# A two-layer macaron decoder on one core: closing additions and squares ahead of turned tiles' second parts, copies and later splits; the sixth attention unit split ahead of the seventh

## The chip, the cores and the metric

The kernel runs on one core of a Trainium2 chip. The metric is the device time of one execution in microseconds (us). Engines are named as in the profile: PE (TensorE; PEld its weight loads), DVE (VectorE), ACT (ScalarE), POOL (GpSimd) and SP (SyncE, which issues most transfers).

## What is computed

Two layers over 512 tokens of width 1024, all in float32, and a final RMSNorm:

```python
for l in range(DEPTH):                                   # 2
    x = x + 0.5 * swiglu(rms_norm(x, ffn1_norm[l]), ffn1_wg[l], ffn1_wu[l], ffn1_wd[l])   # 1024 -> 2816 -> 1024
    h = rms_norm(x, mix_norm[l])
    z = h @ w_in[l]                                      # q (8 heads), k, v (2 heads), three conv parts
    attn_out = sliding_window_attention(q, k, v, attn_sink[l])   # window 128, blocks of 128
    conv_out = short_conv(b, c, h_conv, conv_w[l])       # depthwise, 3 taps
    x = x + concatenate([attn_out, conv_out]) @ w_out[l]
    x = x + 0.5 * swiglu(rms_norm(x, ffn2_norm[l]), ffn2_wg[l], ffn2_wu[l], ffn2_wd[l])
return rms_norm(x, final_norm)
```

## The kernel before

**Exact products from split operands.** Every operand of a product is split in two: `hi` is the operand cast to the matmul's type (a cast on ACT, L214), `lo` the rest (a subtraction on DVE, L215). Three matmuls, hi*hi, lo*hi and hi*lo, stand for one. `need_split(g)` makes the splits of weight tiles up to number g into `wh` and `wl` (four buffers each), `take_split()` takes the next one and asks for those three ahead. The raw tiles (512 KB, eight buffers) are loaded four units ahead, mostly from SP's queue (L198, L193), some with an accumulating transfer from POOL (L209).

**Seven products for eight.** The larger products go block by block in seven products over sums of blocks (`seven`, `Seven`, `share`, `winograd`, `winograd2`; `stream` issues the matmuls, L901). `share` runs through a list of seven steps. After a step its accumulators are added to the residual stream `x` in the additions of L951.

**Closing groups.** Where a normalisation follows directly, `share` gets it as `after` and uses the order `CHAINS_EARLY`. Such closings stand at the end of the first feed-forward part of layer 0 and at the end of the mixed part in each layer. There the first two token tiles (half 0) are complete early: each addition that completes a part of `x` is followed by the square of it with a running sum (`Norm.__call__`, L607, ACT). When four have been squared, `Norm.stage` computes the factor: `v` (L631, DVE), a first guess `r` (L632, ACT), three small DVE steps (L514 to L516), and then four scaled tiles `xn` (L641, DVE). `Norm.pull` and `Norm.turn` transpose an `xn` on PE (L665), cast it on ACT (`hh` or `fb`, L674), subtract on DVE (`hl` or `fb`, L675) and, before a feed-forward part, keep a whole copy (`hf`, L677, ACT). In a closing, half 0 is turned between the matmuls of the last step (`z`); the additions of that step complete half 1.

The next part begins on half 0 while half 1 is still normalised: `halves` (after the first closing; PE L333, three weight tiles held) or `plain_halves` (after the mixed parts; PE L1060, four tiles held). Both take their weight tiles first, and `pull` half 1 at fixed places between their matmuls, so PE's order is written out by hand there. The order of DVE and ACT is set by a scheduler from the order in the program; `tc.issue_after(i)` places what is in it behind instruction `i` in that order, without a wait at run time.

**The first feed-forward part of layer 0** has one pair of column blocks done in `winograd`, after a `winograd2`. At the end of `winograd2`, `apart` copies the 16-bit halves of four result tiles into planes on ACT (L1158), `send` has SP transpose them (L1164) and `join` copies them back (L1218) some steps later. At the start of `winograd`, ACT copies the first product `p` out of its accumulator (L1095), and the third step accumulates into the same bank (L1111).

**Attention.** There are eight units, (query block, key head), and each has steps in a table: scores, then either `turn` (transposes on PE, cast L1578, subtraction L1579) or `send` and `join` (planes on ACT L1540, transposed by SP L1547, copied back on ACT L1560, cast `ph` L1564, subtraction `pl` L1566), then `values` (PE, L1590 and L1591). `go_on` does the values, turns, sends and scores of a step, then the next weight split, then the joins:

```python
TURN_AT = (6, None, 8, None, 11, None, 14, 15)
SEND_AT = (None, 7, None, 9, None, 11, None, None)
JOIN_AT = (None, 10, None, 12, None, 14, None, None)
VALUES_AT = (7, 11, 9, 13, 12, 15, 15, 16)
```

The sixth unit is joined in step 14, where the seventh is turned, and both have their values in step 15.

## Time and profile before

| | |
|---|---|
| time, median of 3 runs | 1648.42 us (1647.46 to 1648.55) |
| profiled execution | 1652.75 us, its span 1651.0 us |
| PE busy | 1634.2 us, 99% of the span |
| DVE, ACT busy | 1299.8 us (79%), 1126.2 us (68%) |
| granted PE clock over the span | 0.997 |
| transfers | 308.64 MB, mean 187 GB/s |

The profile is of one execution. Rows of a timeline give start and duration in us, engine, line of the kernel, operation, what is written and read, the count of merged instructions, and in brackets the idle time of the engine before it with what ended that. The durations of PE's matmuls are modelled and overlap; how fast PE runs is read from the distance of their starts. Instructions of DVE and ACT overlap by about 0.1 us as well.

### The profile page before, as it was taken

The page shows a single profiled execution, that of the slowest core. Times are in us where ns is not written, and L with a number is a line of the kernel's source. Part 1 is how long each engine was busy: PE and PEld are TensorE (multiplying, and loading weights), DVE is VectorE, ACT ScalarE, POOL GpSimd, SP SyncE. Part 2 cuts the span into 40 slices and gives each one's busy share as a digit, 9 for nine tenths or more (in the row PEclk, how much of TensorE's full clock was granted, in tenths as well). Part 3 has the DMA queues.
Part 4 walks back from the last instruction along what each step waited for, and adds up shares of the span by engine and source line. Part 5 has one row for each costly group of instructions (what it writes and reads, how often), then busy time and mean ns, then how long its engine had stood idle before and what let it go on. Part 6 is the DMA issues. An engine that isn't in the chain of part 4 may idle for free.

```text
span 1651.0 us, 21081 instructions
## 1 busy us (share of the span) xinstructions
PE 1634.2 (99%) x7576; PEld 1358.5 (82%) x7576; DVE 1299.8 (79%) x1718; ACT 1126.2 (68%) x1581; POOL 193.1 (12%) x172
## 2 busy tenths in 40 slices
PE   9999999999999999999999999999999999999998
PEld 7888888888887888888888888878988878888886
DVE  7987779877798877798788676987577987777885
ACT  7457777557866667786576777865587766777864
POOL 0011111100111111111001111110002101111111
PEclk9999999999999999999999999999999999999999
DMA  9379999932685779999837898997137847999992
GB/s 255 91 190 221 227 210 258 219 91 52 172 198 128 204 193 215 217 228 243 230 83 198 217 217 204 234 242 200 52 90 175 207 114 183 221 219 222 221 259 79
DMA packets 286844, 308.64 MB, mean 187 GB/s; under 512 B 108532, under 2 KB 171028, under 8 KB 286740
## 3 DMA queue, kind: packets, MB, share of 16 engines
q1 hardware_dynamic: 244212, 227.99, 47.4%
q0 software_dynamic: 41824, 78.65, 28.1%
q8 instruction: 59, 0.97, 0.2%
q10 hardware_dynamic: 704, 0.66, 0.1%
q14 instruction: 45, 0.37, 0.1%
HBM read 263.74 MB, written 2.10 MB: 161 GB/s over the span
## 4 chain that ended last, share of the span: by engine, by line
PE 85%; DVE 6%; ACT 4%; DMA 3%; issue 1%; SPq 1%; DVEq 0%; ACTq 0%; POOLq 0%
PE x L901 23%; PE y L901 12%; PE x_s L901 8%; PE w L901 6%; PE y_s L901 4%; PE up L1060 3%; PE down L356 3%; PE acc L306 3%; PE acc L307 3%; PE acc L309 3%; DVE wl L215 2%; PE w_s L901 2%; PE acc L333 2%; DMA raw<-in_ffn_wu_dram 2%; PE x_m L901 1%
## 5 line engine op out<-in xcount | busy, mean ns | idle before, releaser
L215 DVE TENSOR_TENSOR wl<-raw,wh 128x1024 fp32r<-128x1024 f32 (+1 forms) x493 | 595.5, 1214 | 219.2 <-ACT wh L214 216.0
L214 ACT CAST wh<-raw 128x1024 fp32r<-128x1024 f32 (+1 forms) x493 | 511.7, 1044 | 312.9 <-PE y L901 41.3
L901 PE MATMUL x<-wh,ft 128*128 128x512 f32 x608 | 187.1, 389 | 0.0
L901 PE MATMUL y<-wh,ft 128*128 128x512 f32 x608 | 187.1, 389 | 0.0
L901 PE MATMUL x<-wh,fb 128*128 128x512 f32 x608 | 187.1, 389 | 0.0
L901 PEld LDWEIGHTS y<-wh,ft 128*128 128x128 f32 x608 | 114.1, 188 | 23.6
L901 PEld LDWEIGHTS x<-wh,fb 128*128 128x128 f32 x608 | 114.1, 188 | 23.6
L901 PEld LDWEIGHTS x<-wh,ft 128*128 128x128 f32 x608 | 114.1, 188 | 23.6
L901 PE MATMUL x<-wl,fb 128*128 128x512 f32 x304 | 118.3, 389 | 0.0
L901 PE MATMUL x<-wl,ft 128*128 128x512 f32 x304 | 118.3, 389 | 0.0
L901 PE MATMUL y<-wl,ft 128*128 128x512 f32 x304 | 118.3, 389 | 0.0
L1218 ACT COPY raw_a<-pt 128x1024 uint16<-128x1024 uint16 x76 | 103.3, 1359 | 17.1 <-DMA pt<-pl 17.1
L209 POOL DMA_DIRECT2D raw<-in_ffn_wu_dram x39 | 47.3, 1221 | 553.6 <-DMA raw<-in_ffn_wu_dram 373.5
L306 PE MATMUL acc<-hh,wh 128*128 128x512 f32 x240 | 94.6, 394 | 0.0
L307 PE MATMUL acc<-hl,wh 128*128 128x512 f32 x240 | 93.8, 391 | 0.0
L309 PE MATMUL acc<-hh,wl 128*128 128x512 f32 x240 | 93.7, 390 | 0.0
L901 PE MATMUL w<-wh,fb 128*128 128x512 f32 x304 | 93.6, 389 | 0.0
L901 PE MATMUL x_s<-wh,ft_s 128*128 128x512 f32 x256 | 79.0, 390 | 1.0 <-DVE x L951 0.9
L901 PE MATMUL y_s<-wh,ft_s 128*128 128x512 f32 x256 | 78.8, 389 | 0.0
L242 DVE TENSOR_TENSOR raw<-raw,raw 128x1024 f32<-128x1024 f32 x58 | 70.5, 1220 | 9.1 <-DMA raw<-in_ffn_wd_dram 4.9
L209 POOL DMA_DIRECT2D raw<-in_ffn_wg_dram x39 | 47.2, 1217 | 232.3 <-DMA raw<-in_ffn_wu_dram 95.1
L901 PE MATMUL x_s<-wh,fb_s 128*128 128x512 f32 x240 | 73.9, 389 | 0.0
(364 smaller groups left out, 3422.2 us busy)
## 6 DMA issues: line engine op xcount, KB each, us to landing
raw<-in_ffn_wu_dram SPq DMA_DIRECT2D x120, 512.0 KB, 5.2
raw<-in_ffn_wd_dram SPq DMA_DIRECT2D x104, 512.0 KB, 7.0
raw<-in_ffn_wg_dram SPq DMA_DIRECT2D x80, 512.0 KB, 5.1
raw<-in_ffn_wu_dram POOLq DMA_DIRECT2D x39, 512.0 KB, 8.8
raw<-in_ffn_wg_dram POOLq DMA_DIRECT2D x39, 512.0 KB, 6.4
raw<-in_w_in_dram SPq DMA_DIRECT2D x36, 512.0 KB, 4.7
raw<-in_ffn_wd_dram POOLq DMA_DIRECT2D x32, 512.0 KB, 8.5
raw<-raw POOLq DMA_DIRECT2D x20, 512.0 KB, 8.7
```

The source lines that it names most:

```text
L209: nc.gpsimd.dma_start(out=r, in_=rows_of(*more), accum_op=ALU.add)
L214: cast = nc.scalar.copy(hi, raw)
L215: state["sub"] = eng.tensor_sub(lo, raw, f32(hi))
L242: nc.vector.tensor_add(a11, a11, s1)
L306: nc.tensor.matmul(acc, hi[:, k, :], rhs[k][0], start=k == first, stop=False)
L307: nc.tensor.matmul(acc, hi[:, k, :], rhs[k][1], start=False, stop=False)
L309: nc.tensor.matmul(acc, lo[:, k, :], rhs[k][0], start=False, stop=k == last)
L333: nc.tensor.matmul(accs[j][:, t * H : (t + 1) * H], w[:, k, :], x_, start=t + k + i == 0, stop=k == KC - 1 and i == 2, skip_group_check=True,)
L356: nc.tensor.matmul(acc, a[:, k, tok], w[:, k, :], start=i + k + n == 0 and fresh[t], stop=i == last and k == 1 and n == 2, skip_group_chec ...
L901: nc.tensor.matmul(accs[u], x_[:, 2 * h + k, tok], w[:, k, :], start=start and h + k + i == 0, stop=h + k == 2 and i == 2, skip_group_chec ...
L1060: nc.tensor.matmul(accs[t], x_[:, tok], w[:, k, :], start=j + k + i == 0, stop=j == 3 and k == 1 and i == 2,)
L1218: nc.scalar.copy(room.rearrange("p c (n z) -> p c z n", z=2)[:, :, z, :], turned[0][:, NT * z + 2 * c : NT * z + 2 * c + 2, :],)
```

## The change

It makes four moves; the instructions stay the same, and so does PE's order.

- In a closing, the second part of a turned tile is put off. For the first pair of tiles (o = 0) the subtraction stays and the `hf` copy waits; for the second pair (o = 1) both wait. They are kept in `after.later` and issued by `go_on`: subtractions behind the closing additions, `hf` copies behind the squares.
- The weight splits that follow are put later. From step 4 of a closing, `share` asks for one split less ahead; the one of step (6, 1) goes behind the turned subtractions. A new `hold` in `halves` and `plain_halves` places the third held tile's split behind the last closing addition and the fourth's behind the first pair of `xn`.
- `winograd2` ahead of `winograd` (block "u") keeps back the plane copies of its last two tiles until the first product of `winograd` has been copied out.
- `JOIN_AT` keeps the sixth unit alone and is done after the values and before the turns of its step; the second and fourth unit, in `LATE_JOIN_AT`, stay behind the split.

In the order that results, DVE has, before a feed-forward part: two `fb` subtractions, the second held split, the two closing additions, two `fb` subtractions, `v`, the third held split, the rest of the factor, four `xn`, the fourth held split. Before, it had: two held splits, four `fb` subtractions, a held split, the additions, the last held split, `v` and the rest. On ACT the two squares come ahead of the four `hf` copies, two of which stand before the guess `r`. In attention the two join copies of the sixth unit (L1560) move on ACT from behind a later weight cast (`wh`) to between two `ph` casts of the fourth unit, and its `ph` and `pl` ahead of the seventh unit's. On SP one raw load moves ahead of the last two plane transposes of the first feed-forward part; POOL's order stays.

```diff
-JOIN_AT = (None, 10, None, 12, None, 14, None, None)
+JOIN_AT = (None, None, None, None, None, 14, None, None)
+LATE_JOIN_AT = (None, 10, None, 12, None, None, None, None)
...
+    def hold(norm, n):
+
+        first = state["group"]
+        if norm.added:
+            for ahead, one in ((2, norm.added), (3, norm.first)):
+                with behind(one):
+                    need_split(first + ahead)
+        return [take_split(SPLIT_AHEAD - j)[1:] for j in range(n)]
+
     def halves(norm, n, done):
 
         first = state["group"]
-        held = [take_split(SPLIT_AHEAD - j)[1:] for j in range(n)]
+        held = hold(norm, n)
...
             newton(y, r, v)
+            self.first = None
             for o in range(2):
                 xns = []
+                self.first = self.first or (self.scaled if o else None)
...
             nc.scalar.copy(hi, tp)
-            nc.vector.tensor_sub(lo, tp, f32(hi))
-            if not self.mixing:
-                nc.scalar.copy(self.full[o][:, :, tok], tp)
+
+            def rest():
+                self.turned = nc.vector.tensor_sub(lo, tp, f32(hi))
+
+            def keep():
+                if not self.mixing:
+                    nc.scalar.copy(self.full[o][:, :, tok], tp)
+
+            if self.later is None:
+                rest()
+                keep()
+            elif o:
+                self.later.extend(((rest, "added"), (keep, "squared")))
+            else:
+                rest()
+                self.later.append((keep, "squared"))
+
+        def go_on(self):
+
+            for do, behind_ in self.later:
+                with behind(getattr(self, behind_)):
+                    do()
+            self.later = None
...
-                held_back = after and (step, h) == (5, 1)
-                with behind(after.guess, after.scaled) if held_back else nullcontext():
-                    _, wh, wl = take_split(
-                        SPLIT_AHEAD - 1 if after and step in (4, 5) else SPLIT_AHEAD
-                    )
+                held_back = {(5, 1): ("guess", "scaled"), (6, 1): ("turned",)} if after else {}
+                with behind(*(getattr(after, n) for n in held_back.get((step, h), ()))):
+                    _, wh, wl = take_split(SPLIT_AHEAD - 1 if after and step >= 4 else SPLIT_AHEAD)
+                if after and (step, h) == (6, 0):
+                    after.later = []
...
-                            nc.vector.scalar_tensor_tensor(
+                            added = nc.vector.scalar_tensor_tensor(
                                 part, accs[acc][m], by * sign, part, op0=ALU.mult, op1=ALU.add
                             )
                         if after and (step, (o, t)) in ENDS_EARLY:
                             after(2 * t + m, o)
+                        if after and step == 6 and m:
+                            after.added = added
+                            after.go_on()
...
-            held = [take_split(SPLIT_AHEAD - j)[1:] for j in range(4)]
+            held = hold(norm, 4)
...
                     if step == 0:
-                        keep("p1", m, out)
+                        kept_last = keep("p1", m, out)
+                        for lay in pending.pop("u", ()) if m else ():
+                            with behind(kept_last):
+                                lay()
...
             def apart(t):
 
+                if then == "u" and t > 1:
+                    pending.setdefault("u", []).append(lambda: lay(t))
+                else:
+                    lay(t)
+
+            def lay(t):
+
                 planes.append(g2(f"pl_{name}_{t}", U16, (P, 2, S)))
...
-                self.far = JOIN_AT[NT * g + n]
+                self.far = SEND_AT[NT * g + n]
...
-        def attend(step, what=(VALUES_AT, TURN_AT, SEND_AT, SCORES_AT)):
+        def attend(step, what=(VALUES_AT, JOIN_AT, TURN_AT, SEND_AT, SCORES_AT)):
...
-            attend(step - 1, (JOIN_AT,))
+            attend(step - 1, (LATE_JOIN_AT,))
```

More of the change, by code (lines that the diff above doesn't have):

```diff
@@ L116, in g8, with behind @@
         return work.tile(list(shape), dt, tag="g8", bufs=4, name=name)
+    def behind(*those):
+        stack = ExitStack()
+        for one in those:
+            if one is not None:
+                stack.enter_context(tc.issue_after(one.ins))
+        return stack
     def parts_of(name):
@@ L571, in __init__ @@
             self.seen = [0, 0]
+            self.later = self.added = None
             if mixing:
@@ L605, in __call__ @@
         def __call__(self, t, o):
-            nc.scalar.activation(
+            self.squared = nc.scalar.activation(
                 junk(f"sq_{self.i}_{t}_{o}"),
@@ L910, in stream @@
                 norm.pull()
-    def behind(*those):
-        stack = ExitStack()
-        for one in those:
-            stack.enter_context(tc.issue_after(one.ins))
-        return stack
     def share(
@@ L1094, in keep @@
                     kept[what] = g2(f"{what}_{name}", F32, (P, 2, H))
-                nc.scalar.copy(kept[what][:, m, :], src)
+                return nc.scalar.copy(kept[what][:, m, :], src)
             for step, (acc, operand, start) in enumerate(CHAINS):
@@ L1150, in winograd2 @@
             turned = {}
+            then = stages[at + 1][0]
             def apart(t):
+                if then == "u" and t > 1:
[3 more added lines that the diff above has]
+            def lay(t):
                 planes.append(g2(f"pl_{name}_{t}", U16, (P, 2, S)))
@@ L1226, in part @@
                     split(*acts[b + c], raws[b][:, 2 * c : 2 * c + 2, :])
-            gap = 1 if stages[at + 1][0] in "dw" else 2
+            gap = 1 if then in "dw" else 2
             plan = [(1 + n, send, n) for n in range(NT)]
```

## The prediction

> **What bounds the kernel now.** I read the page first, then TensorE's waits, then the timeline of each engine around each wait.

> ```profile
> span 1651.0 us, 21081 instructions
> PE 1634.2 (99%) x7576; PEld 1358.5 (82%) x7576; DVE 1299.8 (79%) x1718; ACT 1126.2 (68%) x1581; POOL 193.1 (12%) x172
> PE 85%; DVE 6%; ACT 4%; DMA 3%; issue 1%; SPq 1%; DVEq 0%; ACTq 0%; POOLq 0%
> ```

> TensorE is busy for 1634.2 of 1651.0 us, and the chain that ended last is 85% its own. The order of its instructions does not move in this change, so all there is to win or lose is its stalls. The view of TensorE's waits (engine, line, releaser; us, times, longest) names them:

> ```profile
> PE xt L665 <- DVE xn L641: 3.8, 3, 1.7
> PE o L1591 <- DVE pl L1566: 1.4, 2, 0.7
> ```

> There are five places: the closing of the mixed part of layer 0 (506 us), of layer 1 (1322 us) and of the first feed-forward part (345 us), where transposes L665 wait for the normalised tiles `xn`; the seventh product step of attention in each layer (445 and 1262 us); and one place in the first feed-forward part (235 us, below). The windows view tells what such a stall costs beside its own length. Its columns are us, then busy time of PE, PEld, DVE, ACT and POOL, then granted clock, DMA share, GB/s:

> ```profile
> 506.90:509.90 3.00, 1.28 (x11) 0.85 (x9) 2.53 (x8) 0.70 (x2) 0.00 (x0) 1.00 1.00 299
> 509.90:514.20 4.30, 4.30 (x15) 3.39 (x13) 1.97 (x4) 1.94 (x4) 2.41 (x2) 0.60 0.59 125
> 1325.90:1330.00 4.10, 4.10 (x13) 3.20 (x12) 1.77 (x3) 1.76 (x3) 2.41 (x2) 0.58 0.47 102
> 235.00:237.00 2.00, 1.01 (x9) 0.80 (x8) 1.76 (x3) 2.00 (x6) 0.00 (x0) 1.00 0.93 253
> ```

> After the two long stalls the granted clock is 0.60 over 4.30 us and 0.58 over 4.10 us: 0.40 x 4.30 = 0.42 x 4.10 = 1.7 us lost each time behind the stall. After the stall of 235 us, which leaves 1.0 us of 2.0 idle, the clock stays at 1.00.

> **The closings of the mixed part.** TensorE in layer 0 (start, us; the x24 and x8 rows are from the chain that ended last and give the undisturbed pace):

> ```profile
> 501.22 0.91 PE L1060 MATMUL up<-wh,fb 128*128 128x512 f32 x2
> 506.76 0.39 PE L1060 MATMUL up<-wl,fb 128*128 128x512 f32 x1
> 508.83 1.29 PE L665 MATMUL xt<-ident,xn 128*128 128x128 f32 x8 [1.68 <-DVE xn L641]
> 515.09 0.71 PE L1060 MATMUL up<-wh,fb 128*128 128x512 f32 x2
> ...
> 514.46 0.87 PE xt L665 x8
> 528.95 5.44 PE x L901 x24
> ```

> A matmul takes 5.44 / 24 = 0.227 us. Between 501.22 and 515.09 lie 36 of them (8.16) and two sets of transposes (1.74), 9.90 us of work in 13.87 us: 3.97 us are lost. In them are 1.84 (508.83 less 506.76 + 0.23), 1.7 for the clock, 0.3 at the start, where the `fb` split is late, and 0.2 where the second `xn` is late. VectorE sets all of this:

> ```profile
> 498.63 2.35 DVE L215 TENSOR_TENSOR wl<-raw,wh 128x1024 fp32r<-128x1024 f32 x2
> 500.89 2.48 DVE L675 TENSOR_TENSOR fb<-xt,fb 128x512 fp32r<-128x512 f32 x4
> 503.29 1.22 DVE L215 TENSOR_TENSOR wl<-raw,wh 128x1024 fp32r<-128x1024 f32 x1
> 504.42 1.28 DVE L951 SCALAR_TENSOR_TENSOR x<-z_m,x 128x512 f32<-128x512 f32 x2
> 505.62 1.22 DVE L215 TENSOR_TENSOR wl<-raw,wh 128x1024 fp32r<-128x1024 f32 x1
> 506.75 0.16 DVE L631 TENSOR_TENSOR v<-ss 128x2 f32<-128x2 f32 x1
> 507.27 0.17 DVE L635 TENSOR_SCALAR v<-v 128x2 f32<-128x2 f32 x1 [0.36 <-ACT r L632]
> 507.93 2.74 DVE L641 SCALAR_TENSOR_TENSOR xn<-x,y,gain 128x512 f32<-128x512 f32 x4
> ...
> 502.15 2.04 ACT L677 COPY hf<-xt 128x512 f32<-128x512 f32 x4
> 506.50 0.19 ACT L607 ACTIVATION_READ_ACCUMULATOR sq<-x 128x1 f32 x1
> ```

> VectorE runs without a gap but the 0.36 us that it waits for ScalarE's `r`. A weight split takes 1.13 from start to start, an `fb` split or an addition 0.60. The changed order after the first split of 498.63 is: two `fb`, the second split, both additions, the other two `fb`, `v`, the third split, then `v`, `y`, `xn`, and only then the fourth split. I lay it out with these durations. The `fb` splits start at 499.76, so the first is done at 500.45, before TensorE asks (501.22): the 0.3 us go. The split follows at 500.96, the additions at 502.09 instead of 504.42, which is 2.33 earlier, the two `fb` at 503.29. The squares end at 506.68 - 2.33 = 504.35. `v` comes at 504.49 and the third split at 504.57, done at 505.79. On ScalarE two `hf` copies (0.5 each) now stand between the squares and `r`: `r` starts at 505.35 and is done by 505.65, still inside the third split, so they cost nothing; that cover is only some 0.1 us, and beyond it each us of ScalarE would be a us of `xn`. The second `v` starts at 505.70 and `xn` 0.66 later, at 506.36 instead of 507.93. Checked in another way: 507.93 less the fourth split (1.13) less the filled wait (0.36) is 506.44.

> What is late next: TensorE, without its 0.3, asks for `xn` at 506.69 and can start 0.15 after the first `xn` ends (507.11), at 507.26. So 0.57 us of the stall stay, and 0.2 us for the second `xn`, which comes 0.67 after the first when four transposes take 0.44. No clock drop is to be expected from 0.8 us, since 1.15 us at 235 us brought none. The third split (505.79) is needed behind the transposes, about 508.6; the fourth, now at 509.05 to 510.27, one tile of 12 matmuls and a set of transposes later, about 512. The buffers these splits free let two loads start later by 1.3 and 3.4 us; the queue behind them next has the transposes of 531 us, so this is nothing. Gain in layer 0: 3.97 - 0.8 = 3.2.

> ```profile
> 1316.77 0.39 PE L1060 MATMUL up<-wh,fb 128*128 128x512 f32 x1
> 1330.88 0.71 PE L1060 MATMUL up<-wh,fb 128*128 128x512 f32 x2
> ```

> Layer 1 loses 14.11 - 9.90 = 4.21. Its `xn` waits are the same to 0.1; I leave it 1.0 and take a gain of 3.2. Both: 6.4 (6.2 to 8.2, the latter if no stall stays).

> **The closing of the first feed-forward part.** Here the second stage works in 256-column matmuls, and the held tiles are wanted sooner:

> ```profile
> 336.26 2.36 DVE L215 TENSOR_TENSOR wl<-raw,wh 128x1024 fp32r<-128x1024 f32 x2
> 343.21 0.28 PE L333 MATMUL acc<-hh,wl 128*128 128x256 f32 x1
> 346.47 1.29 PE L665 MATMUL xt<-ident,xn 128*128 128x128 f32 x8 [0.46 <-DVE xn L641]
> ```

> The loss is 0.46, plus 0.16 because a matmul's modelled end (0.39) overhangs its pace (0.23), plus 0.2 for the second `xn`: 0.8. In the new order: `hl` splits from 337.39, the second split 338.60, additions 339.73, `hl` 340.93, squares done 2.26 after the additions began (506.68 - 504.42), 341.99, but at the latest by 342.3, since ScalarE has a weight cast before them; `v` 342.3, the third split 342.4 to 343.62. TensorE wants that third split at 343.21 and gets it at 343.77: a new stall of 0.56, with `v` and its wait for the squares ahead of it in VectorE's queue. It pushes the transposes back by as much, and `xn` (from 344.2) is then in time. Gain 0.8 - 0.6 = 0.2, between 0 and 0.8.

> **The deferred plane copies** (235 us).

> ```profile
> 235.02 1.14 ACT L1158 COPY pl<-p 128x512 uint16<-128x512 uint16 x2
> 236.48 0.50 PE L1111 MATMUL x<-ft,wh 128*128 128x256 f32 x2 [0.99 <-ACT p L1095]
> ```

> TensorE waits until ScalarE has copied `p` out of the bank, and four plane copies (2 x 1.14) stand before that. With them behind the `p` copies these end about two us earlier, before 235.3. 0.99 + 0.16 = 1.15 goes. The planes themselves are complete at about 236.2 in either order, so their transposes on SP's queue are not late; one load moves ahead of two of them. Next late is the `u` copy, which has over a us. Gain 1.15, at worst 0.

> **The sixth attention unit**, joined at step 14 ahead of the seventh unit's turn.

> ```profile
> 443.28 1.28 DVE L1579 TENSOR_TENSOR pl<-pt,ph 128x512 fp32r<-128x512 f32 x2
> 446.58 0.50 PE L1591 MATMUL o<-pl,vv 128*128 128x512 f32 x1 [0.68 <-DVE pl L1566]
> ...
> 431.57 0.51 ACT L1517 ACTIVATE p<-p,nm 128x256 f32<-128x256 f32 x1 [2.32 <-DVE nm L1511]
> L1560 ACT COPY p<-pr x12: 1337/1350/1369, 409.3 to 1252.6; 128x1024 uint16<-128x1024 uint16 x12
> 422.81 2.61 SPq L1547 DMA_TRANSPOSE pr<-pr  x2
> DMA to landing us min/median/max: 3.2/3.2/3.3
> 432.54 0.39 PE L1591 MATMUL o<-pl,vv 128*128 128x512 f32 x1
> ```

> The splits of the sixth unit take the place of the seventh's at 443.28 and are ready 1 us before TensorE asks (445.5); the seventh's follow by 445.5, wanted 0.9 us after the sixth's. 0.68 + 0.16 = 0.84 goes in each layer, 1.7 in all. The same edit sends the two join copies `p<-pr` forward, between two `ph` casts of the fourth unit. That stretch of ScalarE held 2.32 us of idle time, and the copies take 2 x 1.35 less overlap, 2.55. The second `ph` then ends at 431.7 and its split at 432.4, against TensorE at 432.54: covered, with about nothing over. Their transposes were sent by 424.1 and land 3.2 later, at 427.3, before the copies start at 428.6.

> **Sum.** 3.2 + 3.2 + 0.2 + 1.15 + 1.7 = 9.45, taken as 9.4. The profiled execution took 1652.75 (span 1651.0 and 1.75 around it); it would take 1643.3. The median of the runs shown, 1648.42, is 4.3 less; the stalls are set by engine order, not by transfers, so I take the same 9.4 from it: **1639.0**. If every stall named goes, 3.97 + 4.21 + 0.8 + 1.15 + 1.7 = 11.8, and it is 1636.6.

> **Rivals.**
> *The clock stays.* If the stalls are cut but the low clock still comes, twice 1.7 is not won: 6.0, so 1642.4. Two of two long stalls had the drop right behind them, which speaks against it; that it starts over a us after the stall ended, and that the runs without a profile may have had none, speaks for it. [...] Chance 0.13.
> *A wait takes the place.* `v` heads VectorE's queue while it waits for the squares, and `r` stands behind two `hf` copies. If this takes back the 1.6 us of `xn`, the closings gain nothing and 1.15 + 1.7 = 2.85 is left: 1645.6. The cover of 0.1 us speaks for it, and that each us of delay would have to come at both closings against it. Chance 0.10. That the moves have no effect at all (1648.4): 0.03.
> *Slower.* The join copies sit in ScalarE's queue ahead of a `ph` that TensorE needs; if their transposes land late, all waits. From 424.1 + 3.2 there are 2.5 us in hand, so up to 5.7 us to land it costs nothing. Beyond it each us is a us of TensorE, and a long stall adds 1.7, in both layers. From some 9 us it eats the 9.4; with 10.6 us, 2 x (4.9 + 1.7) = 13.2, 3.8 more than the gain: 1652.2. Against it: all twelve landed in 3.2 to 3.3. With other reorderings that cost unseen: 0.10.

> **The numbers.** A change of 0.2%, 3.3 us, is about what a measurement of this kernel tells from none. My forecast has 0.64, around 1639.0 (1636.6 to 1641). Faster: 0.64 + 0.13 and a part of the second rival, 0.80; same 0.10; slower 0.10. The range from 1636.6 up to 1645.0 leaves out the same and the slower.

> **What would show it.** Right: the long waits of L665's transposes under 0.7 us with a granted clock of 1.00 after them; no wait of the `o` matmuls for `pl` nor of the `x` matmuls for the `p` copy; a new wait of about 0.6 us for `wl` near 343. Wrong: a low clock remaining after the closings, ScalarE idle before the moved `p<-pr`, or `r` later than the third split.

## The result and the profile after

The changed kernel takes 1641.44 us (median of five runs, 1641.10 to 1642.01) against 1648.18 us before (1647.10 to 1648.55). The ratio is 0.9961, with a 95% interval of 0.9946 to 0.9975. The gain is 6.7 us; the prediction had 9.4 and 1639.0. In the profiled executions the gain is larger than in the medians: the span went from 1651.0 to 1639.9 us, 11.1 us less. That difference between the two gains is what the experiments are about.

The head of the page of the changed kernel, then TensorE's waits in it (us, times, longest). A line of the kernel before stands some 20 to 50 lines further down here, so L665, L641, L1060, L901 have become L685, L661, L1097, L941:

```profile
span 1639.9 us, 21080 instructions
PE 1629.8 (99%) x7576; PEld 1356.7 (83%) x7576; DVE 1300.8 (79%) x1718; ACT 1128.7 (69%) x1581; POOL 193.5 (12%) x172
PE 92%; DVE 4%; ACT 1%; DMA 1%; issue 1%; SPq 0%; ACTq 0%; DVEq 0%
```

```profile
PE idle L151 <- DVE warm L785: 1.2, 1, 1.2
PE xt L685 <- DVE xn L661: 0.8, 2, 0.4
PE acc L350 <- DVE wl L223: 0.5, 1, 0.5
PE y_m L941 <- ACT wh L222: 0.3, 1, 0.3
```

Of the five places named in the prediction three are empty: no `x` waits for the `p` copy, no `o` for `pl`, and the first closing no longer waits for `xn`. The two mixed closings keep 0.4 us each in this view, where it was 1.7, and one wait is new, 0.5 us for `wl`. The 0.3 us for `wh`, at 481 us, need not come from the change: one run further down that has the old order there (`stall_4us`) shows it as well. TensorE's own part of the chain that ended last rose from 85% to 92%.

VectorE at the mixed closing of layer 0, and TensorE's two rows around the stall that is left (start, us, work, idle before it):

```profile
499.35 1.22 DVE L223 TENSOR_TENSOR wl<-raw,wh 128x1024 fp32r<-128x1024 f32 x1
500.48 1.29 DVE L985 SCALAR_TENSOR_TENSOR x<-z_m,x 128x512 f32<-128x512 f32 x2
501.68 1.29 DVE L697 TENSOR_TENSOR fb<-xt,fb 128x512 fp32r<-128x512 f32 x2
502.87 0.16 DVE L649 TENSOR_TENSOR v<-ss 128x2 f32<-128x2 f32 x1
502.94 1.23 DVE L223 TENSOR_TENSOR wl<-raw,wh 128x1024 fp32r<-128x1024 f32 x1
...
504.74 2.74 DVE L661 SCALAR_TENSOR_TENSOR xn<-x,y,gain 128x512 f32<-128x512 f32 x4
507.39 1.22 DVE L223 TENSOR_TENSOR wl<-raw,wh 128x1024 fp32r<-128x1024 f32 x1
```

```profile
504.83 0.39 PE L1097 MATMUL up<-wl,fb 128*128 128x512 f32 x1
505.64 1.29 PE L685 MATMUL xt<-ident,xn 128*128 128x128 f32 x8 [0.42 <-DVE xn L661]
```

The order is the one laid out in the prediction, and there is no gap on VectorE. From start to start TensorE has 0.81 us where a matmul takes 0.23, so 0.58 us of the stall stay; 0.57 were forecast. ScalarE's `r` ran from 503.60 to 503.90, inside the third split (502.94 to 504.17), so the two `hf` copies ahead of it cost nothing: the cover was 0.27 us.

The new wait, in the first closing:

```profile
341.98 0.28 PE L350 MATMUL acc<-hl,wh 128*128 128x256 f32 x1
342.78 0.39 PE L350 MATMUL acc<-hh,wl 128*128 128x256 f32 x1 [0.52 <-DVE wl L223]
```

0.80 us from start to start at a pace of 0.12: 0.68 are lost, where the prediction had 0.56. The stalls are as predicted, so the term to suspect is the clock. The windows view of the changed kernel shows only that it is 1.00 behind the closing (columns as in the prediction):

```profile
505.00:508.41 3.41, 2.96 (x17) 2.25 (x17) 3.41 (x5) 1.17 (x2) 0.00 (x0) 1.00 1.02 232
508.41:511.82 3.41, 3.41 (x21) 2.90 (x20) 2.27 (x5) 2.30 (x5) 1.01 (x1) 1.00 0.67 212
```

### The profile page after: what moved, and what is told of

The parts are those of the page before. It is cut to its first block, busy times and chain, and to the rows that moved or that the text cites. A ratio compares the mean times of both kernels' runs of the same rounds, so it can differ in the third digit from the quotient of the medians.

```text
span 1639.9 us, 21080 instructions
## 1 busy us (share of the span) xinstructions
PE 1629.8 (99%) x7576; PEld 1356.7 (83%) x7576; DVE 1300.8 (79%) x1718; ACT 1128.7 (69%) x1581; POOL 193.5 (12%) x172
## 4 chain that ended last, share of the span: by engine, by line
PE 92%; DVE 4%; ACT 1%; DMA 1%; issue 1%; SPq 0%; ACTq 0%; DVEq 0%
PE x L941 25%; PE y L941 13%; PE x_s L941 10%; PE w L941 6%; PE y_s L941 5%; PE down L373 3%; PE acc L314 3%; PE acc L315 3%; PE acc L317 3%; PE up L1097 3%; PE w_s L941 3%; PE acc L350 2%; DVE wl L223 1%; PE acc L839 1%; DMA raw<-in_w_out_dram 1%
## 5 line engine op out<-in xcount | busy, mean ns | idle before, releaser
L941 PE MATMUL y<-wh,ft 128*128 128x512 f32 x608 | 187.3, 389 | 0.0
L941 PE MATMUL x<-wh,fb 128*128 128x512 f32 x608 | 187.3, 389 | 0.0
L941 PE MATMUL x<-wh,ft 128*128 128x512 f32 x608 | 187.3, 389 | 0.0
L941 PEld LDWEIGHTS x<-wh,ft 128*128 128x128 f32 x608 | 114.1, 188 | 23.7
L941 PEld LDWEIGHTS x<-wh,fb 128*128 128x128 f32 x608 | 114.1, 188 | 23.7
L941 PEld LDWEIGHTS y<-wh,ft 128*128 128x128 f32 x608 | 114.1, 188 | 23.7
L941 PE MATMUL y<-wl,ft 128*128 128x512 f32 x304 | 118.3, 389 | 0.0
L941 PE MATMUL x<-wl,fb 128*128 128x512 f32 x304 | 118.3, 389 | 0.0
L941 PE MATMUL x<-wl,ft 128*128 128x512 f32 x304 | 118.3, 389 | 0.0
L1266 ACT COPY raw_a<-pt 128x1024 uint16<-128x1024 uint16 x76 | 103.2, 1358 | 11.1 <-DMA pt<-pl 11.1
L941 PE MATMUL w<-wh,fb 128*128 128x512 f32 x304 | 93.6, 389 | 0.0
L941 PE MATMUL x_s<-wh,ft_s 128*128 128x512 f32 x256 | 78.8, 389 | 0.0
L941 PE MATMUL y_s<-wh,ft_s 128*128 128x512 f32 x256 | 78.8, 389 | 0.0
L941 PE MATMUL x_s<-wh,fb_s 128*128 128x512 f32 x240 | 73.9, 389 | 0.0
```

The lines of the kernel that those rows point to most:

```text
L941: nc.tensor.matmul(accs[u], x_[:, 2 * h + k, tok], w[:, k, :], start=start and h + k + i == 0, stop=h + k == 2 and i == 2, skip_group_chec ...
L1266: nc.scalar.copy(room.rearrange("p c (n z) -> p c z n", z=2)[:, :, z, :], turned[0][:, NT * z + 2 * c : NT * z + 2 * c + 2, :],)
```

## Experiments

The theory to test: the low clock behind the two long stalls, 2 x 1.7 us, was in the one execution that the profile shows, and not in those that make the median. The rival: it was in all of them, and the changed kernel loses 2.7 us elsewhere.

**The kernel before, once more.** No edit.

> The kernel before, unchanged, once more with a profile. Theory P (the profile shown was a slower execution than the median: the low clock behind the two long stalls and some of its other losses are not in every execution): ratio 1.000; a new profile has a span near 1646.5 instead of 1651.0, a mean clock above 0.997 and at most one of the two stretches of 0.60 and 0.58. Rival C (the low clock follows the 1.84 us stall every time, and the missing 2.7 us of gain are lost elsewhere in the changed kernel): the new profile has the two stretches again, mean clock 0.997.

1648.71 us, ratio 1.0007 (0.9998 to 1.0016); the profiled execution took 1648.33 us with a span of 1646.6, 4.4 less than the one shown at first. Its stalls at the mixed closings are the same:

```profile
PE xt L665 <- DVE xn L641: 3.8, 3, 1.7
PE x L1111 <- ACT p L1095: 1.7, 1, 1.7
PE o L1591 <- DVE pl L1566: 1.3, 2, 0.7
```

But the clock behind them is not:

```profile
507.84:511.25 3.41, 1.71 (x12) 1.37 (x12) 3.12 (x8) 1.08 (x3) 0.00 (x0) 1.00 0.99 326
511.25:514.67 3.42, 3.42 (x21) 2.89 (x20) 1.37 (x3) 1.97 (x5) 2.41 (x2) 1.00 0.38 61
```

In the same layout the execution shown at first has this:

```profile
506.88:510.30 3.42, 1.70 (x12) 1.21 (x11) 2.95 (x9) 1.02 (x3) 0.00 (x0) 1.00 0.99 308
510.30:513.71 3.41, 3.41 (x10) 2.63 (x9) 1.57 (x3) 1.61 (x3) 2.41 (x2) 0.50 0.48 86
1322.67:1326.08 3.41, 1.71 (x12) 1.20 (x11) 2.94 (x9) 1.00 (x3) 0.00 (x0) 1.00 0.99 314
1326.08:1329.49 3.41, 3.41 (x10) 2.63 (x9) 1.59 (x3) 1.63 (x3) 2.41 (x2) 0.50 0.36 77
```

Cut this way, the low stretches are exactly one piece of 3.41 us at half clock: 10 matmuls where the other execution has 21. Where a profile has more than one change of the granted clock to go by, they lie on a grid of 3.41 us: these two low pieces begin 815.78 us apart, 239 times 3.413, and in `stall_4us` (below) low pieces begin 167.26, 498.35 and 993.28 us after the first, 49, 146 and 291 times. The position of the grid against the kernel differs from one execution to the next: it has a border at 506.88 us here and at 507.84 in the repeat, counted back 333 steps from the fall of the clock at its end (1644.5). A piece, below, is one step of that grid. The piece before each of these two low ones holds the whole stall and about half a piece of work (1.70 and 1.71 us).

The mean granted clock that each execution has on record says how often this happens. It is 0.999 in all seven profiles without a low piece and 0.998 or less in the five that have one. Of the 33 executions of the kernel before that ran beside this one, 20 have 0.999 (median 1647.5 us), 12 have 0.998 (1649.8 us) and one, the slowest, has 0.997, as the one shown at first. All ten executions of the changed kernel have 0.999. So the rival falls, and the theory stands with one addition, an estimate from these clocks: some four in ten executions of the kernel before have a low piece, seldom two, and more than half have none. Where these pieces lie is not known for executions without a profile. Measured against the repeat, the span of the changed kernel is 1646.6 - 1639.9 = 6.7 us shorter, as in the medians.

**One part at a time.** First the closings alone: the diff without its `JOIN_AT` lines and without the kept-back plane copies.

```diff
-                if then == "u" and t > 1:
+                if False:
```

> The kernel before with the closings' part of the change alone (additions and squares ahead, hold). Theory P: the stalls won are 1.84 + 0.3 + 0.2 less 0.8 in layer 0, 1.83 + 0.44 + 0.2 less 0.8 in layer 1 and about 0.1 in the first feed-forward part, 3.3 us in all, ratio 0.998. Rival C: the low clock goes as well, 3.4 more, 6.7 us, ratio 0.996.

1644.34 us against 1648.18, ratio 0.9976 (0.9967 to 0.9984): 3.8 us, near the 3.3 without the clock and far from 6.7.

Then the plane copies alone, the kernel before with `apart`, `lay` and `kept_last` of the diff.

> The kernel before with the plane copies of the last two tiles behind the copies of the first product, and nothing else. Both theories: the wait of 1.15 us at 235 us goes, 1648.2 to 1647.0, ratio 0.9993. If the saving is given back later: 1.0000.

1646.99 us, ratio 0.9993 (0.9983 to 1.0003), 1.2 us less; the interval includes none. In the profile the wait is gone, which by itself proves little, as the next experiment shows.

Then the sixth unit alone, the kernel before with the `JOIN_AT` and `LATE_JOIN_AT` lines.

> The kernel before with the sixth unit's join ahead of the seventh's turn, and nothing else. Theory P: the two waits of 0.84 us go, 1.7 us, ratio 0.9990. Rival C (part of the gain is lost here, by the join copies in front of the fourth unit's cast): 0 to 0.5 us, ratio 0.9997 to 1.0000, and a wait of the o matmuls for the fourth unit's split near 432 us.

1646.63 us, ratio 0.9990 (0.9981 to 0.9999), 1.5 us less. The three parts add up to 3.8 + 1.2 + 1.5 = 6.5 of the 6.7 us. The 0.2 us by which this one stays under the forecast can be seen in the profiles: with the new order the last `o` matmul of the stage starts late in both layers (0.44 us behind the one before it in the changed kernel, at 452.99 and 1262.76, where the pace is 0.23), since VectorE's split for it does not come forward as far as TensorE does.

These profiles also show the wait at 235 us, where it is not removed, with another length each time: 1.0 in the one shown first, 1.7 in the repeat, 1.9 here, 3.0 with the closings alone. What sets the length is a load. VectorE's sum of two raw tiles ahead of the `u` tiles waits for it, everything up to ScalarE's `p` copy is late by that, and the wait on VectorE is as long as the one on TensorE: 1.05, 1.71, 1.91 and 3.03 us in the same order. In the stall runs further down it is 1.23 us once, with 1.2 on TensorE, and once the load is in time and TensorE does not wait, although the plane copies stand where they did. The first row is that of the execution shown first, the second with the closings alone, the third of a run with the plane copies moved (`no_later`, below):

```profile
225.35 1.23 DVE L249 TENSOR_TENSOR raw<-raw,raw 128x1024 f32<-128x1024 f32 x1 [1.05 <-DMA raw<-in_ffn_wu_dram]
227.45 1.23 DVE L256 TENSOR_TENSOR raw<-raw,raw 128x1024 f32<-128x1024 f32 x1 [3.03 <-DMA raw<-in_ffn_wu_dram]
226.37 1.23 DVE L257 TENSOR_TENSOR raw<-raw,raw 128x1024 f32<-128x1024 f32 x1 [1.94 <-DMA raw<-in_ffn_wu_dram]
```

In the profiles of the changed kernel and of the plane copies alone the load was in time. It is the third row that shows the move at work: the load is late by 1.94 us, and TensorE does not wait (nor in `no_hold`, with 1.41). So the length of this wait is that of the load's delay, and the move covers at least 1.9 us of delay.

Twice a half-clock piece follows the wait. The first two rows are those of the kernel with the sixth unit alone, then those with the closings alone:

```profile
235.62:239.03 3.41, 1.56 (x13) 1.50 (x13) 2.62 (x5) 3.41 (x8) 0.00 (x1) 1.00 1.20 232
239.03:242.44 3.41, 3.41 (x18) 3.41 (x17) 2.72 (x3) 3.01 (x6) 1.20 (x1) 0.50 1.19 160
```

```profile
235.29:238.70 3.41, 0.44 (x4) 0.24 (x3) 2.52 (x4) 3.41 (x8) 0.00 (x0) 1.00 1.13 298
238.70:242.11 3.41, 3.41 (x17) 3.41 (x18) 2.62 (x4) 3.20 (x7) 1.20 (x1) 0.50 1.00 162
```

**Longer stalls.** The kernel before, with the first `xn` of the second half written several times over, three times in the first run (below) and five times in the second:

```diff
-                    self.scaled = nc.vector.scalar_tensor_tensor(
...
+                    for _ in range(3 if half and not o and t == at else 1):
+                        with tc.issue_after(last.ins) if last else nullcontext():
+                            self.scaled = nc.vector.scalar_tensor_tensor(
...
+                        last = self.scaled if half else None
```

Theory W's 1.8 us without work is an estimate from the pieces above: 3.41 - 1.56 = 1.85 us brought a low piece in the run of the sixth unit alone, 1.7 brought one twice in the execution shown at first and none in the repeat.

> The kernel before with the first xn of the second half computed three times over in the closings (same values), so that each of the three stalls grows by 2 x 0.66 us: 1.84 to 3.2 twice, 0.62 to 1.95 once. Theory W (TensorE's clock is judged in windows of 3.41 us, one after the other: a window with more than about 1.8 us without work makes the next one half as fast, 1.7 us lost; a 1.84 us stall seldom fits, one of 3.2 us nearly always leaves that much in one window): low stretches of 3.41 us behind both long stalls, time + 4.0 + about 2 x 1.5 + some of the third = 6.5 to 8.5 us, ratio 1.0040 to 1.0052. Rival R (a low stretch follows a stall by chance, whatever its length): + 4.0 us, ratio 1.0024, and a low stretch in at most one place.

1657.80 us (1654.43 to 1663.46) against 1647.78, ratio 1.0063 (1.0045 to 1.0081). The rival's 1.0024 is out; theory W's 1.0052 is within the interval, but the median is 1.5 us above its range. One reason is a miss of mine: normalisations at two more places turn half 1 with the same code, and they stall now too (1.4 us at 837 and 0.3 at 1163; lost time from start to start). With 1.6 more at each of the three intended places that is 6.5 us of stalls. The other 3.5 us of the median go with the clock: the four executions took 1654.43, 1657.41, 1658.19 and 1663.46 us, with mean granted clocks of 0.998, 0.996, 0.996 and 0.994. Only the fastest was profiled, and it has one low piece; the others must have more. The two long stalls of that profile show why the number varies:

```profile
507.09:510.51 3.42, 0.61 (x3) 0.19 (x1) 2.88 (x9) 0.45 (x3) 0.00 (x0) 1.00 1.06 312
510.51:513.92 3.41, 2.96 (x11) 2.76 (x12) 3.26 (x6) 1.57 (x3) 1.87 (x2) 0.50 0.21 77
1322.88:1326.29 3.41, 1.75 (x8) 1.13 (x6) 2.91 (x9) 1.53 (x5) 0.00 (x0) 1.00 1.10 256
1326.29:1329.70 3.41, 1.79 (x11) 1.48 (x12) 3.37 (x6) 1.09 (x2) 1.21 (x1) 1.00 0.54 205
```

The stall of layer 0 (507.54 to 510.9) fell almost whole into one piece and left it 0.61 us of work: half clock next. The stall of layer 1 is as long, 3.4 us, but a border cut it in the middle; each piece kept 1.75 and 1.79 us of work, and the clock stayed.

> As the one with the first xn three times over, but five times: stalls of 4.5, 4.5 and 3.3 us. Theory W: a low stretch behind each of the three, sometimes of two windows: + 7.9 + 3 x 1.7 to 3 x 2.1 = 13 to 14.5 us, ratio 1.0079 to 1.0088. Rival R: + 7.9, ratio 1.0048.

1669.20 us (1666.49 to 1672.63), ratio 1.0123 (1.0108 to 1.0139), 21.4 us more, above both. The stalls that can be seen grew by 14.6 us, since the two other places stall here by 3.2 and 1.9 us; and in the profiled execution, the slowest of the four, each of the four longest has a low piece behind it, and those behind 345 and 1339 us are followed by another. Its mean granted clock of 0.991 fits two behind each: 0.009 x 1670.8 = 15.0 us are lost, 8 x 1.7 = 13.6 and the fall at the end. One of the four:

```profile
1338.94:1342.35 3.41, 0.00 (x0) 0.00 (x0) 3.17 (x8) 0.00 (x1) 0.00 (x0) 1.00 0.95 299
1342.35:1345.76 3.41, 2.08 (x9) 2.10 (x10) 3.37 (x6) 0.69 (x2) 1.87 (x2) 0.50 0.11 37
1345.76:1349.18 3.42, 3.42 (x9) 2.64 (x8) 1.06 (x2) 1.57 (x3) 0.54 (x1) 0.50 1.04 172
```

The first low piece still begins with the rest of the stall, so at half clock it does 2.08 / 2 = 1.0 us' worth of work, and the next is low again. Theory W had a second piece only "sometimes"; this and the two further stalls are where its estimate fell short.

**Which part of the closings wins.** The changed kernel, once with the held splits asked for as before, once with the turned parts done at once as before.

```diff
-        if norm.added:
+        if False:
...
-                held_back = {(5, 1): ("guess", "scaled"), (6, 1): ("turned",)} if after else {}
+                held_back = {(5, 1): ("guess", "scaled")} if after else {}
...
-                    _, wh, wl = take_split(SPLIT_AHEAD - 1 if after and step >= 4 else SPLIT_AHEAD)
+                    _, wh, wl = take_split(SPLIT_AHEAD - 1 if after and step in (4, 5) else SPLIT_AHEAD)
```

> The changed kernel with the held weight splits asked for as before the change (three of them ahead of the additions, the fourth ahead of the factor); additions and squares still stand ahead of the later turned parts. Theory H (the splits put off bring most of what the closings win): VectorE saves only the two fb subtractions ahead of the additions, part of it lost again while v waits; the waits for xn at the mixed closings are 1.4 us instead of 0.58, and fb is 0.3 late at their start; the wait for wl near 342 goes, as the third split is early: 1641.5 + 2 x 1.1 - 0.7 = 1643, ratio 0.9972. Rival A (additions and squares first bring most): waits for xn stay under 0.8, 1641 to 1641.5, ratio 0.996.

1644.05 us against 1648.20, ratio 0.9980 (0.9969 to 0.9991), 1.0 us above the 1643 expected; the other expectation, 0.996, is out. Lost time at the `xn` waits of the mixed closings: 1.38 and 1.39 us, 1.4 expected. The wait for `wl` near 342 goes, as expected, but the transposes at 345 wait for `xn` again, and by 355 us TensorE has given back 0.6 of the 0.8 us won there, which is about half of the 1.0.

```diff
-                if after and (step, h) == (6, 0):
-                    after.later = []
...
-                            after.go_on()
```

> The changed kernel with the turned tiles' second parts done at once, ahead of additions and squares, as before the change; the held splits still put off. Theory H: the additions come 1.2 us later than in the changed kernel, but the third split then stands ahead of v, so xn is only 0.3 us later: waits for xn of 0.9 us, no wait for wl near 342: 1641.5 + 2 x 0.35 - 0.7 = 1641.5, ratio 0.9962. Rival A: waits for xn of 1.6 to 1.8, 1643.5, ratio 0.9974.

1642.36 us, ratio 0.9961 (0.9947 to 0.9975). The interval holds both expectations, 0.9962 and 0.9974; the waits decide. Lost at the `xn` waits: 1.00 and 1.01, where 0.9 was expected, and 1.6 to 1.8 by the rival. The wait for `wl` near 342 was expected to go and only fell to 0.41. The rows of the `xn` waits, without the held splits and then without the later turned parts:

```profile
506.74 0.52 PE L685 MATMUL xt<-ident,xn 128*128 128x128 f32 x3 [1.21 <-DVE xn L661]
```

```profile
506.00 1.18 PE L685 MATMUL xt<-ident,xn 128*128 128x128 f32 x7 [0.83 <-DVE xn L661]
```

So of the 1.26 us that the stall of layer 0 lost (1.84 to 0.58), the additions ahead bring 0.46 by themselves and the splits put off 0.84 by themselves. Moving the weight splits does more than what the title names first, and the times agree: 2.6 us are lost without it, 0.9 without the other.

**Another order.** What is left is VectorE's order, so I ordered the closings once more. The first lines are for closings ahead of a feed-forward part: the third held split goes behind the first two `xn`, and `scale_rest` makes the last two. The later lines put the turned parts behind `v`.

```diff
+        elif norm.added:
+            with behind(norm.added):
+                need_split(first + 1)
+            with behind(norm.first):
+                need_split(first + 2)
+            with behind(state["sub"]):
+                norm.scale_rest()
+            with behind(norm.scaled):
+                need_split(first + 3)
...
+                for do in put_off:
+                    with behind(self.summed):
+                        do()
+                last = self.turned
+            with behind(last):
+                nc.vector.tensor_scalar(v, v, 1.0 / D, EPS, op0=ALU.mult, op1=ALU.add)
```

> The changed kernel with the closings ordered once more. Mixed closings, on VectorE: two fb, one fb of the second pair, both additions, the second held split, v, the last fb, factor, the first two xn, the third held split, the last two xn, the fourth; ScalarE's r ahead of all hf copies. First closing: the third held split ahead of v, the last two hl behind v. Theory (what is left of the stalls is VectorE's order alone): the additions start about 0.5 us and xn about 1.1 us earlier than in the changed kernel, so the waits of 0.58 and 0.56 us for xn and 0.68 us for wl near 342 go, with 0.2 more at each mixed closing: 2.2 us under the changed kernel, ratio to the kernel before 0.9946. Rival (the split now put between the xn pairs is wanted first): a wait of 0.3 to 0.6 us for wl takes their place, no gain over the changed kernel, ratio 0.996.

1639.26 us (1638.47 to 1639.69) against 1647.78, ratio 0.9947 (0.9934 to 0.9959). The changed kernel ran beside it:

> The changed kernel unchanged, once more, beside the others of this call: ratio 0.996, the same waits of 0.58, 0.56 and 0.68 us, no low clock before the end.

1641.57 us (1641.33 to 1642.44), ratio 0.9962 (0.9950 to 0.9975). The new order is 2.3 us faster than the change, 2.2 expected, and no run of the one overlaps the other. All three waits are gone:

```profile
498.23 1.28 DVE L1013 SCALAR_TENSOR_TENSOR x<-z_m,x 128x512 f32<-128x512 f32 x2
499.42 1.22 DVE L223 TENSOR_TENSOR wl<-raw,wh 128x1024 fp32r<-128x1024 f32 x1
500.56 0.16 DVE L658 TENSOR_TENSOR v<-ss 128x2 f32<-128x2 f32 x1
...
501.88 1.42 DVE L681 SCALAR_TENSOR_TENSOR xn<-x,y,gain 128x512 f32<-128x512 f32 x2
```

```profile
503.10 0.39 PE L1125 MATMUL up<-wl,fb 128*128 128x512 f32 x1
503.33 1.03 PE L712 MATMUL xt<-ident,xn 128*128 128x128 f32 x8
```

The transposes start 0.23 us after the last matmul, at the undisturbed pace: the row of the first two `xn` ends at 503.30, before they begin.

## Why the prediction was right, and where it was off

**Right, and by its own steps.** The stalls. `xn` of layer 0 was put at 506.36 in the time of the kernel before; by then the changed kernel runs 1.6 us ahead, which makes 504.76, and it came at 504.74. Left of the stall: 0.57 forecast, 0.58 measured. First closing: a new stall of 0.56 forecast, 0.68 measured, with the cause named (`v` and its squares ahead of the third split). Plane copies: 1.15 forecast, 1.2 measured, in an interval that includes none. Sixth unit: 1.7 forecast, 1.5 measured; the second `ph` behind the moved join copies was put at 431.7, 430.5 after the 1.2 us gained by then, and ended at 430.50. Without the clock the sum of the prediction is 9.4 - 3.4 = 6.0, and 6.7 was measured (between 4.1 and 8.9 by the interval of the ratio).

**Right with some luck.** The main forecast, with its 0.64, stood on 1636.6 to 1641, and 1641.44 lies just above that. It lies inside the range up to 1645 because that made room for the rivals.

**Off: the clock term of both closings.** The two times 1.7 us in "3.2 + 3.2" were read correctly from the profile shown, and the change does take them away there: the span fell by 11.1 us, some 7.2 of it stalls over 0.25 us and 3.4 the clock. But they were not in the median. In these profiles the clock fell only behind a piece of the grid with 1.71 us of work or less, about half, and this stall leaves about that where it falls whole into one piece (1.68 us of wait, 3.41 - 1.68 = 1.73). Even then the clock stayed once with 1.71 us of work in the piece and fell once with the same 1.71; with the stall cut by a border, at 1320 us in the repeat, the piece kept 1.79 and the clock stayed. In the six stalls of this kind whose kernels were run later with a profile (the repeat, and the two parts alone) it never brought a low piece; in the two of the execution shown at first it did both times. The prediction saw that this execution took 4.3 us more than the median, and still took all 9.4 from the median, because "the stalls are set by engine order, not by transfers". Those of the closings and of attention are; what follows from them is not, and the one at 235 us takes its length from a late load, so its 1.15 was a figure of one execution too. That 1.2 was measured for it in the median is in part luck. The two low pieces (3.4) and a wait in the second layer behind a late transfer, which no edit touches and the repeat does not have (1.5 from start to start), less what the repeat loses more at 235 us (0.7), make 4.2 of the 4.4 us between the two spans. The changed kernel's profile does not have that wait either, so it is in the 11.1 us without being the change's doing. That wait, at VectorE and then at TensorE:

```profile
1102.74 1.23 DVE L242 TENSOR_TENSOR raw<-raw,raw 128x1024 f32<-128x1024 f32 x1 [1.28 <-DMA raw<-in_ffn_wd_dram]
```

```profile
1104.71 0.70 PE L901 MATMUL x_s<-wh,ft_s 128*128 128x512 f32 x2 [0.88 <-DVE x L951]
1105.75 0.50 PE L901 MATMUL x_s<-wl,ft_s 128*128 128x512 f32 x1 [0.34 <-DVE wl L215]
```

**The rivals.** "The clock stays" gave 1642.4, nearest to what came, and one of its reasons (the runs without a profile may have had none) is what the repeat and the recorded clocks showed; its condition, that the clock still falls in the changed kernel, did not come. That the drop starts over a us after the stall ended, its other reason, is the grid: in layer 0 the stall was over at 508.83 us and the clock fell at the next border, 510.30. The two other rivals did not come: `r` stayed inside the third split, and no join waited for its transposes.

## What to carry to other kernels

Here a stall that an engine's order sets was a fact of the kernel (the waits for `xn` were 3.8 us in all, the longest 1.7, in each of four profiles with the old closings), but a stall whose chain starts at a late load (none to 3.0 us), and a drop of the clock behind a stall, were facts of one execution: before either goes into a sum made against a median, look at how the profiled execution stands to the median and at the mean granted clock of the others, and price the drop by how likely the stall is to fall whole into one piece of the grid (3.41 us here). Where one engine paces a hand-over, list what stands ahead of it and ask of each piece when it is wanted. Here work that is wanted late (weight splits) was worth more to move than the work on the path itself, and an order that also splits the hand-over in two (two `xn`, a split, two `xn`) took the rest; which of its moves did so was not separated.

## What the runs showed of the hardware

```profile
349.07:352.48 3.41, 2.47 (x12) 2.50 (x13) 3.35 (x6) 1.08 (x2) 0.00 (x0) 0.50 0.00 0
352.48:355.90 3.42, 3.42 (x19) 3.42 (x18) 0.69 (x1) 0.59 (x2) 0.00 (x0) 0.50 0.00 0
```

- A load from the same place in the program came in time in one execution and up to 3.03 us late for VectorE in others of the same order, and TensorE's wait at 235 us was none to 3.0 us accordingly. The change only covers the lateness; why the load is late by so different amounts was not settled.
